# Low parts of all expert weights on VectorE, indirect transfers alone on GpSimd

## The chip, the cores and the metric

The kernel runs on one core of one Trainium2 chip. The metric is the device time of one execution in microseconds (us), the median of several runs.

## The reference

One decoder block over 2048 tokens of width 1024, in float32: RMSNorm, one input projection, dilated-window attention beside an mLSTM, an output projection, a cross-attention to 256 memory tokens, a mixture of experts, and a final norm. The change touches the mixture of experts. A router gives each token one of four groups and two of the four experts in it. Cut to what matters:

```
glog, elog -> g_idx, top_i, e_w                    # group, two experts, two weights
xb = h_pad[row_tok].reshape(nblk, 128, D)          # tokens sorted by expert
y  = (silu(xblk @ w1[e]) * (xblk @ w3[e])) @ w2[e] # w1, w3: 1024x512, w2: 512x1024
out = zeros.at[row_tok].add(y * row_w)
x  = rms_norm(x + out, g_final)
```

## The kernel before, in words

**Three products for one.** A float32 product is made from three matmuls on a shorter float type (fp32r). Each operand is split into a high part (a cast, on ScalarE) and a low part (operand minus high part, a subtraction of two SBUF tiles). `split` (lines 35 to 44) issues both: line 38 is the cast on ScalarE, line 39 the subtraction on the engine that the caller names. For token tiles that come out of PSUM with a gain, lines 41 and 42 do the same; line 42 reads one PSUM and one SBUF tile, always on VectorE. So in the profile every "L39" instruction is a low part: on weights (128x512 each), or on the gated activations (`actl`).

**An expert.** `experts` (from line 1532) treats 16 experts in order of their token counts, counted from 0 here; expert j has room for C tokens, CAPS = 256 eight times, then 272, 288, 288, 320, 320, 352, 352, 384. For each expert:
- `gather`: indirect transfers on GpSimd's queue fetch token rows to tiles X.
- `turn`: PE transposes X by 128x128 blocks (line 1576), and lines 41 and 42 split the result to xh and xl, eight tiles.
- `up(q)`, q = 0 and 1: for each of two blocks f of 128 features, 24 matmuls with w1 and 24 with w3 (lines 875 to 877) into PSUM tiles `pa`, of which there are four; then silu on ScalarE (line 1628), the product `s` on VectorE (line 1629, which frees the two PSUM tiles), and the split to acth and actl (line 1630). An `up(q)` has 2 x 2 x 24 = 96 matmuls.
- `down`: for each tile of up to 128 tokens, two halves c of 12 matmuls of 512 columns (lines 1640 to 1642), scaled to y on ScalarE (c = 0, line 1644) or VectorE (c = 1, line 1646), and added to the result in memory by an indirect transfer on GpSimd's queue (line 1654). The last two experts fetch, add, norm and store rows instead (`update`).

**The weights.** A unit is 128 partitions of 2048 elements: w1 or w3 for one q (tiles ww_0 and ww_1 in the profile, the number is q), or half of w2 (w_0, w_1). `unit` (line 1581) loads 1 MB over SyncE's queue into one of the `raw` buffers, and calls `split` four times, 512 columns each. Four high and four low unit tiles exist, so a unit's tile comes free as PE finishes the unit four before. In `w13` w1's low parts are on GpSimd and w3's on VectorE; in `w2` half 0 is on GpSimd and half 1 on VectorE. Each expert so has 12 weight low parts on either engine. The weights of the next expert are formed while PE works on this one.

**The first expert** is known early. Its w1 and w3 for q = 0 and its w1 for q = 1 are loaded into buffers of the router (`raws`, tile leadw in the profile). The `lead` branch (lines 1590 to 1596) forms both parts of w1, q = 0, on GpSimd.

**What sets the order.** Each engine runs its instructions in one order, fixed when the program is built by a planner that simulates a time line (line 1867) with its own costs, priority by place in the program. `issue_after` puts instructions behind a given one on its own engine: the next expert's weights for q stand behind the split of the last activation of `up(q)` on ScalarE and VectorE.

Of the kernel before, what the change touches and what calls it, by code (L numbers as in the profile page):

```python
# [16 lines left out]
D = 1024  # L17
# [1514 lines left out]
def experts(tc, I, Z, router, out):  # L1532
    nc = tc.nc
    SP_ = mybir.EngineType.SP
    it = router.finish()
    with ExitStack() as ctx:
# [12 lines left out]
        class Expert:  # L1549
# [51 lines left out]
            def w13(self, q, raws=(None, None)):  # L1601
                cs = slice(q * 256, q * 256 + 256)
                return [self.unit(f"w{m}{self.j}_{q}", I[m][bass.ds(self.e, 1), :, cs].rearrange("o (k p) f -> p (o k) f", p=P), [KT, 256], eng, raw, q == 0 and raw is not None)
                        for m, eng, raw in (("w1", nc.gpsimd, raws[0]), ("w3", nc.vector, raws[1]))]

            def w2(self, q):
                return self.unit(f"w2{self.j}_{q}", I["w2"][bass.ds(self.e, 1), q * 256:q * 256 + 256, :].rearrange("o (k p) d -> p (o k) d", p=P),
                                 [2, D], (nc.gpsimd, nc.vector)[q])

            def up(self, q, w13):  # L1610
                j, C = self.j, self.C
                if q == 0:
                    self.act = [sp.tile([P, 4, self.nt * P], F32R, name=f"act{m}{j}", tag="act" + m, bufs=1) for m in "hl"]
                    if C < self.nt * P:
                        for a in self.act:
                            nc.vector.memset(a[:, :, C:].bitcast(F32), 0.0)
                act = self.act
                for f in range(2):
                    fs = slice(f * P, f * P + P)
                    ps = []  # L1620
                    for m, (wh, wl) in enumerate(w13):
                        p = pa.tile([P, 384], F32, name=f"pa{j}_{q}{f}{m}", tag="a")
                        for k in range(KT):
                            xh, xl = self.xt[k]
                            mm3(nc, p[:, :C], wh[:, k, fs], wl[:, k, fs], xh[:, :C], xl[:, :C], k == 0, k == KT - 1)
                        ps.append(p)
                    s_ = sp.tile([P, 384], F32, name=f"s{j}_{q}{f}", tag="silu")
                    nc.scalar.activation(s_[:, :C], ps[0][:, :C], AF.Silu)
                    nc.vector.tensor_mul(s_[:, :C], s_[:, :C], ps[1][:, :C])  # L1629
                    self.last = split(nc, act[0][:, 2 * q + f, :C], act[1][:, 2 * q + f, :C], s_[:, :C], nc.vector)  # L1630

            def weighted(self, w2, n, r):
                y = sp.tile([P, D], F32, name=f"y{self.j}_{n}", tag="y", bufs=6)
                for c in range(2):
                    ps = py.tile([P, 512], F32, name=f"py{self.j}_{n}{c}", tag="y")
                    cs, ns = slice(c * 512, c * 512 + 512), slice(n * P, n * P + P)
                    for f in range(4):
                        wh, wl = (t[:, f % 2, cs] for t in w2[f // 2])
                        ah, al = (t[:, f, ns] for t in self.act)
                        nc.tensor.matmul(ps, ah, wh, start=(f == 0), stop=False)  # L1640
                        nc.tensor.matmul(ps, ah, wl, start=False, stop=False)
                        nc.tensor.matmul(ps, al, wh, start=False, stop=(f == 3))
                    if c == 0:
                        nc.scalar.activation(y[:r, cs], ps[:r], AF.Copy, scale=self.rt[:r, n, 1:2])
                    else:
                        nc.vector.tensor_scalar(y[:r, cs], ps[:r], self.rt[:r, n, 1:2], None, op0=OP.mult)
                return y

            def down(self, w2):

                added = []
                for n, r in enumerate(self.rows):
                    y = self.weighted(w2, n, r)
                    d = nc.gpsimd.indirect_dma_start(out=Z["acc"], out_offset=bass.IndirectOffsetOnAxis(ap=self.ix[:r, n:n + 1], axis=0),
                                                     in_=y[:r], in_offset=None, compute_op=OP.add)
                    apart(tc, d, added)
# [45 lines left out]
        raws = router.raws + [None]  # L1702
# [168 lines left out]
```

## Time and profile before

| | us |
|---|---|
| median of 3 runs | 2247.65 (2243.78 to 2251.59) |
| the profiled execution's own time | 2247.41 |
| its span, first to last instruction | 2245.2 |
| busy: PE / PEld | 2050.7 / 1884.5 |
| busy: DVE / ACT / POOL | 1389.0 / 1044.3 / 886.2 |

DVE is VectorE, ACT ScalarE, POOL GpSimd, PE the matmuls and PEld the weight loads of TensorE. Times in the rows count from the span's start. A row of a time line is: start, length, engine, line, operation, out<-in, shape, count, and in brackets the idle time before it with what ended it. A row of a table of windows is: stretch, length, then busy time (and instruction count) of PE, PEld, DVE, ACT and POOL, the granted TensorE clock (1.00 is 2.4 GHz, 0.50 is 1.2 GHz), the DMA share and GB/s. Names that end in l are low parts, in h high parts, in r raw weights.

### The profile page before, as it was taken

How to read it: one execution, taken by the hardware profiler on the slowest of the kernel's cores; microseconds unless marked ns; L12 is line 12 of the kernel's file. 1: busy time of each engine (PE TensorE's matmuls, PEld its weight loads, DVE VectorE, ACT ScalarE, POOL GpSimd, SP SyncE). 2: the span in 40 equal slices, each digit the busy share in tenths (PEclk: the TensorE clock that was granted, in tenths of full speed). 3: DMA queues.
4: the chain of work that ended last, by engine and by line, in shares of the span. 5: the costliest groups of instructions: out<-in, count | busy, mean ns of one | idle time of the engine just before them, and what ended most of it. 6: DMA issues, size and time to landing. Idle time of an engine off the chain costs nothing. (4 is left out here: it accounts for less than half of the span.)

```text
span 2245.2 us, 36132 instructions
## 1 busy us (share of the span) xinstructions
PE 2050.7 (91%) x13247; PEld 1884.5 (84%) x13247; DVE 1389.0 (62%) x3127; ACT 1044.3 (47%) x2216; POOL 886.2 (39%) x603
## 2 busy tenths in 40 slices
PE   8999999999789898889788999849998999999995
PEld 6898988988678788889788999749888988889985
DVE  8125641254388888846787888765566656545487
ACT  5213431233267676656535454425544544444453
POOL 3541244411354545542320021155554645455433
PEclk9999999999999999999789999969999999999997
DMA  6553644432897888775631222367667666666686
GB/s 213 165 161 132 225 146 136 132 123 94 213 240 197 242 233 238 194 208 179 227 125 56 95 104 80 114 195 223 209 194 210 199 214 205 169 185 160 175 293 264
DMA packets 276244, 402.45 MB, mean 179 GB/s; under 512 B 28176, under 2 KB 204624, under 8 KB 276016
## 3 DMA queue, kind: packets, MB, share of 16 engines
q1 hardware_dynamic: 262528, 355.11, 51.1%
q0 software_dynamic: 13536, 45.00, 8.1%
q8 instruction: 106, 1.74, 0.3%
q14 instruction: 74, 0.61, 0.1%
HBM read 286.33 MB, written 114.00 MB: 178 GB/s over the span
## 5 line engine op out<-in xcount | busy, mean ns | idle before, releaser
L39 POOL TENSOR_TENSOR wl<-wr,wh 128x1024 fp32r<-128x1024 f32 (+1 forms) x46 | 118.9, 2607 | 256.4 <-ACT wh L38 222.0
L875 PE MATMUL pa<-xh,ww_1h 128*128 128x256 f32 (+5 forms) x512 | 156.3, 305 | 17.1 <-DVE s L1629 17.1
L876 PE MATMUL pa<-xl,ww_0h 128*128 128x256 f32 (+5 forms) x512 | 154.5, 310 | 7.1 <-DVE xl L42 7.1
L876 PE MATMUL pa<-xl,ww_1h 128*128 128x256 f32 (+5 forms) x512 | 155.1, 303 | 0.0
L877 PE MATMUL pa<-xh,ww_1l 128*128 128x256 f32 (+5 forms) x512 | 155.1, 303 | 0.0
L877 PE MATMUL pa<-xh,ww_0l 128*128 128x256 f32 (+5 forms) x512 | 147.8, 302 | 0.0
L334 PE MATMUL pn<-wh,xh 128*128 128x256 f32 (+1 forms) x512 | 144.9, 283 | 0.0
L335 PE MATMUL pn<-wl,xh 128*128 128x256 f32 (+1 forms) x512 | 144.9, 283 | 0.0
L336 PE MATMUL pn<-wh,xl 128*128 128x256 f32 (+1 forms) x512 | 144.9, 283 | 0.0
L875 PE MATMUL pa<-xh,ww_0h 128*128 128x256 f32 (+5 forms) x512 | 133.9, 302 | 3.1 <-ACT xh L41 1.8
L42 DVE SCALAR_TENSOR_TENSOR xl<-pt,f_gf,xh 128x256 fp32r<-128x256 f32 (+5 forms) x128 | 63.9, 513 | 99.4 <-ACT xh L41 91.4
L39 POOL TENSOR_TENSOR ww_0l<-ww_0r,ww_0h 128x512 fp32r<-128x512 f32 x60 | 83.5, 1428 | 102.9 <-ACT ww_0h L38 102.9
L41 ACT ACTIVATE xh<-pt,f_gf 128x256 fp32r<-128x256 f32 (+5 forms) x128 | 62.1, 500 | 129.7 <-PE pt L1576 109.1
L875 PEld LDWEIGHTS pa<-xh,ww_1h 128*128 128x128 f32 x512 | 100.9, 197 | 18.1 <-DVE s L1629 18.0
L39 POOL TENSOR_TENSOR ww_1l<-ww_1r,ww_1h 128x512 fp32r<-128x512 f32 x60 | 85.9, 1452 | 65.0 <-ACT ww_1h L38 37.0
L38 ACT CAST wh<-wr 128x1024 fp32r<-128x1024 f32 (+3 forms) x49 | 48.4, 1030 | 130.6 <-PE pn L336 58.0
L876 PEld LDWEIGHTS pa<-xl,ww_0h 128*128 128x128 f32 x512 | 99.0, 194 | 9.4 <-DVE xl L42 7.3
L39 DVE TENSOR_TENSOR ww_1l<-ww_1r,ww_1h 128x512 fp32r<-128x512 f32 x64 | 102.3, 1654 | 2.4 <-ACT ww_1h L38 2.3
L876 PEld LDWEIGHTS pa<-xl,ww_1h 128*128 128x128 f32 x512 | 100.8, 197 | 0.0
L877 PEld LDWEIGHTS pa<-xh,ww_1l 128*128 128x128 f32 x512 | 100.6, 196 | 0.0
L877 PEld LDWEIGHTS pa<-xh,ww_0l 128*128 128x128 f32 x512 | 98.2, 194 | 1.0
L335 PEld LDWEIGHTS pn<-wl,xh 128*128 128x128 f32 x512 | 97.1, 190 | 0.9
(710 smaller groups left out, 7365.1 us busy)
## 6 DMA issues: line engine op xcount, KB each, us to landing
ww_1r<-w SPq DMA_DIRECT2D x31, 1024.0 KB
ww_0r<-w SPq DMA_DIRECT2D x30, 1024.0 KB
wr<-w_in SPq DMA_DIRECT2D x43, 512.0 KB
w_0r<-w SPq DMA_DIRECT2D x16, 1024.0 KB
w_1r<-w SPq DMA_DIRECT2D x16, 1024.0 KB
z_v<-v SPq DMA_DIRECT2D x32, 256.0 KB
z_mqk<-mq SPq DMA_DIRECT2D x16, 512.0 KB
kk<-z_qkh SPq DMA_DIRECT2D x32, 256.0 KB
```

The lines of the kernel that those rows point to most:

```text
L38: a = nc.scalar.copy(hi, src)
L39: b = eng.tensor_sub(lo, src, hi.bitcast(F32))
L41: a = nc.scalar.activation(hi, src, AF.Copy, scale=scale)
L42: b = eng.scalar_tensor_tensor(lo, src, scale, hi.bitcast(F32), op0=OP.mult, op1=OP.subtract)
L334: nc.tensor.matmul(ps[:, :n], xhw, wh[:, k, :], start=(k == 0), stop=False)
L335: nc.tensor.matmul(ps[:, :n], xhw, wl[:, k, :], start=False, stop=False)
L336: nc.tensor.matmul(ps[:, :n], xlw, wh[:, k, :], start=False, stop=(k == KT - 1))
L875: nc.tensor.matmul(out, wh, xh, start=first, stop=False, skip_group_check=True)
L876: nc.tensor.matmul(out, wh, xl, start=False, stop=False, skip_group_check=True)
L877: nc.tensor.matmul(out, wl, xh, start=False, stop=last, skip_group_check=True)
```

## The change

Every low part of expert weights outside the `lead` branch is issued on VectorE. GpSimd keeps w1, q = 0, of the first expert (the lead branch, high and low part) and the indirect transfers. ScalarE's casts, the loads, the buffers, PE's matmuls and the text order are untouched; the planner fixes the order of the instructions anew.

```diff
@@ -1601,11 +1601,11 @@
             def w13(self, q, raws=(None, None)):
                 cs = slice(q * 256, q * 256 + 256)
                 return [self.unit(f"w{m}{self.j}_{q}", I[m][bass.ds(self.e, 1), :, cs].rearrange("o (k p) f -> p (o k) f", p=P), [KT, 256], eng, raw, q == 0 and raw is not None)
-                        for m, eng, raw in (("w1", nc.gpsimd, raws[0]), ("w3", nc.vector, raws[1]))]
+                        for m, eng, raw in (("w1", nc.gpsimd if q == 0 and raws[0] is not None else nc.vector, raws[0]), ("w3", nc.vector, raws[1]))]
 
             def w2(self, q):
                 return self.unit(f"w2{self.j}_{q}", I["w2"][bass.ds(self.e, 1), q * 256:q * 256 + 256, :].rearrange("o (k p) d -> p (o k) d", p=P),
-                                 [2, D], (nc.gpsimd, nc.vector)[q])
+                                 [2, D], nc.vector)
 
             def up(self, q, w13):
                 j, C = self.j, self.C
```

## Rows read from the trace of the kernel before

**Rows 1.** Windows: the expert stretch, all engines.

```profile
1491.60:2224.00 732.40, 696.80 (x4352) 639.50 (x4352) 437.88 (x669) 355.43 (x714) 364.82 (x274) 0.97 0.69 209
```

**Rows 2.** Windows: experts 2 to 7, then 14 and 15, from up's end to up's end.

```profile
1568.20:1607.40 39.20, 36.78 (x261) 33.88 (x260) 22.69 (x30) 20.32 (x43) 21.67 (x16) 1.00 0.70 210
1607.40:1650.30 42.90, 37.33 (x255) 34.87 (x254) 27.30 (x30) 21.11 (x45) 21.61 (x17) 0.96 0.65 193
1650.30:1688.10 37.80, 36.95 (x262) 34.01 (x261) 21.57 (x30) 19.30 (x41) 20.58 (x16) 1.00 0.75 230
1688.10:1731.60 43.50, 38.17 (x254) 35.72 (x253) 27.24 (x30) 21.60 (x46) 22.31 (x18) 0.92 0.70 202
1731.60:1768.40 36.80, 36.44 (x262) 33.98 (x261) 22.27 (x30) 19.50 (x42) 20.85 (x16) 1.00 0.69 205
1768.40:1810.60 42.20, 37.79 (x255) 35.36 (x253) 27.36 (x30) 20.54 (x44) 21.45 (x17) 0.92 0.65 190
...
2092.70:2142.70 50.00, 50.00 (x290) 46.76 (x289) 28.51 (x46) 26.45 (x51) 19.32 (x14) 1.00 0.63 188
2142.70:2206.80 64.10, 57.61 (x290) 53.15 (x289) 56.84 (x119) 35.57 (x68) 21.55 (x16) 0.92 0.77 278
```

**Rows 3.** Waits of PE in that stretch: us in total, times, longest.

```profile
PE pa L875 <- DVE s L1629: 18.0, 5, 4.4
PE pa L876 <- DVE xl L42: 7.1, 1, 7.1
```

**Rows 4.** Time line of DVE in expert 5.

```profile
1707.36 12.59 DVE L39 TENSOR_TENSOR ww_1l<-ww_1r,ww_1h 128x512 fp32r<-128x512 f32 x4
1719.88 0.74 DVE L1629 TENSOR_TENSOR s<-s,pa 128x256 f32<-128x256 f32 x2
...
1725.73 2.50 DVE L39 TENSOR_TENSOR w_1l<-w_1r,w_1h 128x512 fp32r<-128x512 f32 x4 [4.21 <-ACT w_1h L38]
```

**Rows 5.** Time lines of ACT and of PE there.

```profile
1710.37 0.39 ACT L1628 ACTIVATE s<-pa 128x256 f32<-128x256 f32 x1 [1.48 <-PE pa L877]
...
1720.34 0.58 PE L875 MATMUL pa<-xh,ww_1h 128*128 128x256 f32 x1 [4.31 <-DVE s L1629]
```

**Rows 6.** Time line of POOL there.

```profile
1706.72 3.81 POOL L39 TENSOR_TENSOR ww_1l<-ww_1r,ww_1h 128x512 fp32r<-128x512 f32 x3
1710.70 1.87 POOL L1654 DMA_INDIRECT z_acc<-y,ix  x1 [0.17 <-issue]
...
1713.29 5.51 POOL L39 TENSOR_TENSOR w_0l<-w_0r,w_0h 128x512 fp32r<-128x512 f32 x4
```

**Rows 7.** Tile ww_1l on DVE: shortest, median and longest low part in ns.

```profile
L39 DVE TENSOR_TENSOR ww_1l<-ww_1r,ww_1h x64: 675/1082/7754, 1516.6 to 2190.4; 128x512 fp32r<-128x512 f32 x64
```

**Rows 8.** Groups of DVE: line 42, which reads PSUM and one SBUF tile.

```profile
L42 DVE SCALAR_TENSOR_TENSOR xl<-pt,f_gf,xh 128x256 fp32r<-128x256 f32 x64 | 29.3, 478 | 37.2 <-ACT xh L41 29.2 <-issue 7.9
```

**Rows 9.** Windows of line 39 alone: DVE busy (count), POOL busy (count).

```profile
1491.60:2224.00 732.40, 261.03 (x252) 260.46 (x188) 0.97 0.69 209
```

**Rows 10.** Windows: one up(1) at C = 256 twice, then C = 352 and 320.

```profile
1595.70:1607.40 11.70, 11.70 (x100) 11.70 (x98) 8.44 (x10) 5.86 (x14) 6.64 (x5) 1.00 1.02 313
...
1713.00:1731.60 18.60, 14.29 (x100) 14.09 (x99) 11.63 (x12) 5.86 (x13) 7.18 (x7) 0.82 0.78 221
...
2127.10:2142.70 15.60, 15.60 (x100) 15.58 (x99) 10.34 (x22) 12.31 (x25) 7.05 (x5) 1.00 1.02 371
...
1978.80:1993.00 14.20, 14.20 (x100) 14.19 (x98) 5.41 (x9) 8.60 (x19) 7.92 (x7) 1.00 0.89 291
```

**Rows 11.** Time lines of DVE and POOL in the first expert.

```profile
1511.03 4.57 DVE L1561 CAST ix<-rt 128x3 int32<-128x3 f32 x1 [1.56 <-DMA rt<-z_rt]
...
1510.65 4.92 POOL L39 TENSOR_TENSOR ww_1l<-leadw,ww_1h 128x512 fp32r<-128x512 f32 x4
```

**Rows 12.** Time line of DVE in the last expert.

```profile
2181.30 3.54 DVE L1684 SCALAR_TENSOR_TENSOR fx<-fx,fvf,gfin 128x1024 f32<-128x1024 f32 x2
2184.75 6.35 DVE L39 TENSOR_TENSOR ww_1l<-ww_1r,ww_1h 128x512 fp32r<-128x512 f32 x4
```

**Rows 13.** Waits of DVE, and of PE on ACT, in the expert stretch.

```profile
DVE w_1l L39 <- ACT w_1h L38: 21.7, 9, 4.2
...
PE pa L875 <- ACT xh L41: 1.8, 2, 1.1
```

## The prediction on record

> **What bounds the kernel now.** I read the table of windows first, stage by stage. In the expert stretch, 732.4 us long, PE is busy for 696.8 us [rows 1], and most experts run without a pause: an expert of 256 tokens at its best takes 36.8 us with PE busy for 36.4 of them at clock 1.00 [rows 2]. So the stretch is PE's, and what the change can give is what PE loses beside that. The list of PE's waits names it: 18.0 us in five waits on the product s (line 1629) and 7.1 us in one wait on xl [rows 3], both VectorE's. Neither is long work in itself; both stood late in VectorE's queue.
>
> The time line of one such place shows why. In expert 5 the four w3 low parts begin at 1707.36 and take 12.59 us together; s follows at 1719.88 [rows 4]. The silu that s needs had ended at 1710.37 + 0.39 = 1710.76, and PE stood still for 4.31 us until 1720.34, that is from 1716.03 on [rows 5]. The same four subtractions take 2.50 us at 1725.73 [rows 4], when GpSimd does no low parts. During the 12.59 us GpSimd ran its own: the rest of ww_1l, an indirect transfer, and four of w_0l, ending at 1713.29 + 5.51 = 1718.80 [rows 6]. VectorE's last one gets through only after that. A low part of ww_1l on VectorE takes between 675 and 7754 ns [rows 7]; 7.75 us is more than the whole run of four on GpSimd. Line 42, which reads PSUM and only one SBUF tile, shows no such spread: 478 ns in the mean over the first eight experts [rows 8]. So: a VectorE instruction with two SBUF operands (and in one place a small copy within SBUF, [rows 11]) stands still while GpSimd works through a run of subtractions.
>
> Here a page differs from the row. The Trainium skill (SBUF — State Buffer, "Who interferes with whom") says that a VectorE instruction with two SBUF inputs contends with a GpSimd instruction that reads SBUF, and that the one that starts first holds the pair of ports for its whole instruction. That names the right pair. But by it VectorE would get in after each GpSimd instruction, so a low part would wait for one of them, and four low parts would be done in about 4 x (5.51/4 + 2.50/4) = 8.0 us (an estimate, lengths from rows 4 and 6): s at 1715.4, before PE stops, and no wait to remove. The rows show 12.59 us, and the measurement decides; what the rule would make of the time is the second rival below.
>
> **The change, part by part.** *Removed:* GpSimd's 188 low parts in the stretch, 260.5 us of its time [rows 9]. *Added:* the same 188 on VectorE. There are 252 of line 39 on VectorE now (188 on weights, 64 on activations) for 261.0 us [rows 9]. At the undisturbed 2.50/4 = 0.625 us [rows 4] the 376 weight low parts cost 235 us, and the 64 on activations about 0.45 us each, 29 us (an estimate: below the 0.478 us of line 42 at 256 columns, a bit above for the wider ones). That is 264 us against 261: VectorE's busy time in the stretch stays at some 438 us of 700 [rows 1], although it does twice the low parts.
>
> *Moved, wait by wait.* (a) Experts 2 to 7. Against 36.8 us the six windows are 2.4, 6.1, 1.0, 6.7, 0.0 and 5.4 us longer [rows 2], 21.6 us in all. Three of them hold a wait of about 4.3 us each [rows 3, 5] and the clock that fell with it: in the stalled up(1) 18.6 us against 11.7 us, so 2.6 us beyond the wait, at granted clock 0.82 against 1.00 [rows 10]. After the change eight low parts (5.0 us) from 1707.36 end at 1712.4; even if the four of w_0l stand before s too it runs at 1714.9, before 1716.03. I take the whole 21.6. (b) Experts 8 to 14 show no loss (expert 14: 50.0 us, PE busy 50.0 [rows 2]): nothing to gain. (c) The first expert: a CAST of three columns takes 4.57 us beside GpSimd's w1 low parts of 4.92 us [rows 11], and xl behind it keeps PE for 7.1 us [rows 3]. These low parts now stand on VectorE behind the last xl, so the CAST is short again: 4.4 us back, and of the clock some 1 us, since a wait of 2.7 us (for the list transfers before the CAST) stays: 5.4. (d) The last expert: 64.1 us [rows 2]. Clean it would be the 50.0 of expert 14 and two ups that are 15.6 - 14.2 = 1.4 us longer each for 32 columns more [rows 10], 52.8; so 11.3 us are lost. VectorE is busy for 56.8 us there [rows 2], with the final norm in the same queue. Without GpSimd's low parts it gets back 6.35 - 2.50 = 3.9 us [rows 4, 12] and something on the norm, which two instructions pass in 3.54 us there [rows 12], and it takes 12 x 0.625 = 7.5 us more. VectorE is nearly full there, so I take half, 5.6; bounds 0 and 11.3.
>
> *New waits.* VectorE's queue is in order, so a low part that waits for its cast holds what stands behind it. The trace has that already: nine waits of w_1l, the longest 4.2 us [rows 13], and PE lost nothing by them in the windows without loss. ScalarE makes a cast about as fast as VectorE takes it away, so a unit's four low parts end about one step after its last cast, earlier than the 5.5 us that GpSimd took [rows 6], and raw buffers come free earlier. I charge 2.6 us for small waits of the kind that PE shows on ScalarE now (1.8 us, [rows 13]) and keep 0 and 20 (1.3 us an expert) as bounds. GpSimd's transfers only lose what stood before them.
>
> Sum: 21.6 + 5.4 + 5.6 - 2.6 = 30 us off the profiled execution's 2247.4 (span 2245.2; its time is 0.2 us from the median): **2217 us**.
>
> **Rivals.**
> 1. *VectorE's order becomes the bound (slower).* Place: s in each up(1), behind eight ww_1l (5.0 us) and a wait for w_1's cast as long as the longest, 4.2 us [rows 13]. Slack is 1716.03 - 1710.76 = 5.3 us, so PE stands 3.9 us, with the clock 2.6 more (as in (a)): 6.5 us an expert. It decides from six experts on (6 x 6.5 = 39 against the 32.6 won); with nine of 15 it gives 2247.4 - 32.6 + 58.5 = 2273, with all 15 2312. For it: the order comes from a planner whose costs the trace doesn't show, and 24 low parts an expert now share one queue with s and xl. Against: the best expert has VectorE busy for 22.3 us with 12 low parts [rows 2], and 12 more at 0.625 make 29.8 of 36.8.
> 2. *The two engines pass the ports after each instruction, and the stalls have another cause.* Then the three long waits and the last expert's stay and only the small losses go, 2.4 + 1.0 + 5.4 = 8.8: 2239. Against: 7754 ns [rows 7], and the short CAST that stood still just as long as GpSimd's run [rows 11].
> 3. *Everything comes back*, the last expert too and no new wait: 21.6 + 6.6 + 11.3 = 39.5: 2208, some us lower if the last rows' transfers, no longer behind low parts, start sooner.
> 4. *The loads become the limit.* Stalled experts move 193 GB/s, clean ones 205, and one reached 230 [rows 2]. 43.5 us at 202 are 8.8 MB; at 230 that takes 38.2 us, 1.4 over the best. Over seven experts 10 us come off the gain: 2227.
>
> **The numbers.** Forecast 0.62 (2209 to 2232, with rival 4 inside its upper part), rival 3 0.13, rival 2 and a mixture with small new waits 0.13 (2232 to 2250), rival 1 0.12. Within 0.3%, which is 6.7 us and about what a measurement can tell, lies 2241 to 2254. Rivals 2 and 1 share it: same 0.06; slower 0.10; faster 0.84. The range reaches from 2200 (rival 3 with an earlier end) to 2246, which leaves rival 1 and a part of rival 2 outside.
>
> **What would show it.** Right: weight low parts on VectorE at 0.62 to 0.69 us each with no long ones; line 39 on VectorE near 264 us; PE's wait on s from 18.0 to under 4 us; the windows of experts 3, 5 and 7 near 37 us at clock 1.00; the first expert's CAST at 0.2 us. Wrong: PE waits on s or xl of over 3 us at more than five places, with VectorE's queue held by a low part whose cast is late; or low parts still over 1 us, which would mean that the indirect transfers disturb them as well.

## The result and the profile after

The changed kernel takes **2211.68 us** (median of 4 runs, 2205.8 to 2215.31); the kernel before took 2247.52 (4 runs, 2243.78 to 2251.59). The ratio is **0.9834 [0.9815, 0.9853]**: 35.8 us less, where 2217 was forecast. The profiled execution is the slowest of the four (2215.31 us, span 2213.5; before 2247.4 and 2245.2), so the rows below account for a span difference of 31.7 us.

The windows of the expert stretch after, cut where before's were (up's end to up's end): expert 0, then 2 to 7, 14 and 15, and last the whole stretch with what lies around it. Columns: the window, its length, busy us of PE, PEld, DVE, ACT and POOL, granted clock, DMA share, GB/s.

```profile
1496.30:1532.10 35.80, 30.01 (x213) 28.73 (x214) 19.93 (x53) 18.14 (x38) 10.21 (x11) 0.85 0.78 248
...
1567.90:1603.10 35.20, 35.20 (x254) 33.13 (x253) 20.30 (x40) 17.83 (x38) 5.62 (x4) 1.00 0.74 212
1603.10:1640.00 36.90, 36.72 (x262) 34.11 (x261) 23.64 (x44) 21.10 (x45) 5.48 (x4) 1.00 0.81 236
1640.00:1675.30 35.30, 35.30 (x254) 33.22 (x254) 21.54 (x42) 19.00 (x41) 5.60 (x4) 1.00 0.81 233
1675.30:1711.50 36.20, 36.20 (x261) 34.09 (x260) 24.59 (x46) 22.15 (x48) 5.41 (x4) 1.00 0.81 242
1711.50:1746.70 35.20, 35.20 (x254) 33.14 (x253) 22.51 (x43) 19.55 (x42) 5.51 (x4) 1.00 0.78 226
1746.70:1783.60 36.90, 36.90 (x264) 34.41 (x263) 22.46 (x43) 20.31 (x44) 5.48 (x4) 1.00 0.77 223
2064.10:2114.20 50.10, 50.10 (x290) 46.86 (x289) 27.62 (x59) 25.63 (x49) 4.94 (x3) 1.00 0.65 186
2114.20:2171.20 57.00, 54.59 (x289) 50.54 (x288) 48.95 (x135) 36.45 (x70) 3.35 (x4) 0.97 0.82 305
...
1490.00:2240.00 750.00, 686.93 (x4352) 631.04 (x4352) 432.73 (x909) 356.62 (x717) 124.26 (x97) 0.97 0.70 211
```

Against [rows 2], the 42.9, 43.5 and 42.2 us of experts 3, 5 and 7 have become 36.9, 36.2 and 36.9, with PE busy for all but 0.2 us of any of them, at clock 1.00. Nor did an expert between them keep its 36.8 to 39.2: they take 35.2 or 35.3.

Line 39 alone from the start of the stretch on (VectorE, GpSimd), to be held against [rows 9], and the tile ww_1l, against [rows 7]:

```profile
1496.30:2240.00 743.70, 262.29 (x440) 0.00 (x0) 0.98 0.70 212
```

```profile
L39 DVE TENSOR_TENSOR ww_1l<-ww_1r,ww_1h x124: 616/682/721, 1520.3 to 2150.1; 128x512 fp32r<-128x512 f32 x124
```

Twice the low parts (376 of weights, not 188, beside the 64 of activations) cost VectorE about the same time, 262.29 us for 261.03, since the longest of ww_1l now takes 0.72 us and not 7.75. The time line of VectorE in expert 5, where [rows 4] showed 12.59 us, then in the first and the last expert ([rows 11, 12]):

```profile
1512.20 0.17 DVE L1561 CAST ix<-rt 128x3 int32<-128x3 f32 x1 [0.26 <-DMA rt<-z_rt]
...
1691.17 1.90 DVE L39 TENSOR_TENSOR ww_1l<-ww_1r,ww_1h 128x512 fp32r<-128x512 f32 x3 [3.76 <-ACT ww_1h L38]
...
1695.03 2.49 DVE L39 TENSOR_TENSOR ww_1l<-ww_1r,ww_1h 128x512 fp32r<-128x512 f32 x4
1698.69 0.42 DVE L1629 TENSOR_TENSOR s<-s,pa 128x256 f32<-128x256 f32 x1 [1.17 <-ACT s L1628]
...
2141.75 2.47 DVE L1684 SCALAR_TENSOR_TENSOR fx<-fx,fvf,gfin 128x1024 f32<-128x1024 f32 x2
```

Now s waits for its own silu (1.17 us, expert 5), not for a low part. PE's waits in the stretch, in total, times and longest, against [rows 3]:

```profile
PE pt L1576 <- DMA X<-z_h,ix: 9.9, 2, 8.2
PE pt L1576 <- DVE xl L42: 2.4, 1, 2.4
PE pa L876 <- DVE xl L42: 2.2, 1, 2.2
PE py L1640 <- DVE fv L1681: 2.2, 1, 2.2
...
PE py L1640 <- ACT acth L38: 1.4, 1, 1.4
```

The 18.0 us on s are gone and the 7.1 on xl are 2.2. The 9.9 us at the head is the first gather of X before the first expert; the kernel before has that wait too (8.4 us), and it doesn't explain where the stretch starts: the run that starts first of all (1481.2) has 10.0 us of it.

Where the span went, by stage (us; the start is PE's first transpose of the stage, an expert ends with the last matmul of its second up, the tail runs from the last up's end to the span's end). Most of the experiments discussed below stand in the same table, worked out in the same way from their traces:

```
                    start    e0    e1   e2-7  e8-14   e15   tail
before             1491.6  41.2  35.3  242.5  332.1  64.0   38.5
after              1496.3  35.8  35.8  215.7  330.6  57.0   42.3
control (= after)  1486.1  36.8  35.8  215.1  330.6  55.4   46.1
idle subs, w2      1488.9  42.5  35.8  215.5  330.6  57.8   46.4
memsets            1492.4  36.5  35.8  215.3  330.6  56.3   43.0
w1+w3 on VectorE   1481.2  41.5  35.8  215.1  330.6  56.8   47.3
w2 on VectorE      1487.7  40.9  35.3  226.3  333.8  59.1   44.7
idle subs, all     1490.3  40.3  35.8  232.5  339.1  59.4   50.6
before, own waits  1483.1  40.2  35.4  228.8  339.6  59.5   44.2
low parts twice    1483.0  35.5  38.8  225.4  333.0  58.5   48.9
```

From before to after: start -4.7, expert 0 +5.4, expert 1 -0.5, experts 2 to 7 +26.8, 8 to 14 +1.5, expert 15 +7.0, tail -3.8: 31.7, the span difference. The start scatters between 1481 and 1497 over all the profiles, at a stage that the change does not touch, so single spans are no measure of a few microseconds and the columns of the experts are. Two of the rows come from the fastest execution of their kernel: w1+w3 on VectorE (2210.04 us, median 2220.0) and low parts twice (2225.0, median 2233.85). They show 9 to 10 us less loss than the medians.

### The profile page after: what moved, and what is told of

Same layout as the page of the kernel before. It is cut to its first block, busy times and chain, and to the rows that moved or that the text cites. A ratio compares the mean times of both kernels' runs of the same rounds, so it can differ in the third digit from the quotient of the medians.

```text
span 2213.5 us, 36146 instructions
## 1 busy us (share of the span) xinstructions
PE 2041.5 (92%) x13247; PEld 1875.2 (85%) x13247; DVE 1373.3 (62%) x3315; ACT 1043.4 (47%) x2216; POOL 635.0 (29%) x415
## 5 line engine op out<-in xcount | busy, mean ns | idle before, releaser
L1654 POOL DMA_INDIRECT z_acc<-y,ix x34 | 55.9, 1645 | 407.2 <-DVE y L1646 175.5
L39 DVE TENSOR_TENSOR ww_1l<-ww_1r,ww_1h 128x512 fp32r<-128x512 f32 x124 | 77.6, 676 | 46.3 <-ACT ww_1h L38 46.2
L334 PEld LDWEIGHTS pn<-wh,xh 128*128 128x128 f32 x512 | 97.1, 190 | 0.9
L336 PEld LDWEIGHTS pn<-wh,xl 128*128 128x128 f32 x512 | 96.9, 189 | 0.5
```

What stands on the lines that cost most here:

```text
L39: b = eng.tensor_sub(lo, src, hi.bitcast(F32))
L334: nc.tensor.matmul(ps[:, :n], xhw, wh[:, k, :], start=(k == 0), stop=False)
L336: nc.tensor.matmul(ps[:, :n], xlw, wh[:, k, :], start=False, stop=(k == KT - 1))
```

## The experiments

Theory A: VectorE's two-input instructions are held while GpSimd subtracts; take GpSimd's subtractions away and the gain follows. Theory B: the gain comes from something else that the change moves (the planner's new order, low parts ready sooner, GpSimd's transfers no longer behind subtractions). Each experiment is the changed kernel with an edit, unless it says otherwise; its ratio is to the kernel before on the same chip.

**Control: the changed kernel itself.** No edit.

> The changed kernel once more, beside the next three on the same chip: ratio to the kernel before 0.983 to 0.986.

2209.45 us, 0.9856 [0.9819, 0.9892]. Line 39 takes

```profile
1490.00:2240.00 750.00, 262.24 (x440) 0.00 (x0) 0.98 0.69 209
```

**Idle subtractions on GpSimd.** After each low part of the unit, GpSimd subtracts the high part from itself into one scrap tile that nobody reads; VectorE's own work stays as it is.

```diff
+                        if name[:2] == "w1" or name[:2] == "w2" and name[-1] == "0":
+                            nc.gpsimd.tensor_sub(junk, f(h)[:, cs].bitcast(F32), f(h)[:, cs].bitcast(F32))
```

> The changed kernel, and beside it GpSimd subtracts each 512 columns of the high part of w1 and of the first half of w2 from themselves into a tile that nobody reads: as many subtractions of the same shape, at about the same places, as GpSimd had before the change. VectorE still forms every low part. Theory A (a VectorE instruction with two SBUF operands is held up while a run of GpSimd instructions reads SBUF): the weight low parts on VectorE go from 0.68 us to over 1 us in the mean with the longest over 4 us, PE waits on s and xl again, and the time goes back to 2240 us or above (up to 2275, since 24 low parts an expert are exposed in place of 12). Theory B (the gain came from the new order and from low parts being ready sooner than GpSimd made them): nothing waits for these subtractions, so the time stays at 2212 within 7.

A slip in the edit: w1's units are named "ww1...", so the first test never held, and the 64 subtractions ran for w2's first half only. 2213.66 us, 0.9872 [0.9842, 0.9901]. Line 39 on VectorE, then a place on both engines' time lines:

```profile
1490.00:2240.00 750.00, 301.92 (x440) 0.00 (x0) 0.97 0.69 209
```

```profile
1514.74 5.02 DVE L39 TENSOR_TENSOR ww_1l<-ww_1r,ww_1h 128x512 fp32r<-128x512 f32 x4
...
1513.09 5.51 POOL L1601 TENSOR_TENSOR junk<-w_0h 128x512 f32<-128x512 f32 x4 [5.80 <-ACT w_0h L38]
```

VectorE lost 40 us (301.92 against 262.24 in the control), but in even pieces: beside GpSimd's run three of the four low parts take about 1.52 us, starting and ending in turn with GpSimd's of 1.37 to 1.51, and none longer. That is handing over after each instruction, just what I had argued could not be. In experts 1 to 14 nothing is lost; expert 0 loses what the change had won there (42.5 us against 36.8), with PE waiting 4.4 us for s. So handing over is cheap where s has time to spare, and the long holds need something more. One thing differs from the kernel before besides the place: all these subtractions write one scrap tile, and each starts 0.08 us after the end of the one before, where GpSimd's low parts overlap.

**Writes alone.** The same places (and the same slip), two memsets of the raw tile, some 0.53 us each, in place of the subtraction.

```diff
+                            for _ in range(2):
+                                nc.gpsimd.memset(f(raw)[:, cs], 0.0)
```

> The changed kernel, and beside it GpSimd writes zeros twice over each 512 columns of the raw weights of the same units, after their low part is formed: GpSimd is busy in the same places, but reads nothing. Theory A in its narrow form (only reads of GpSimd hold VectorE up): low parts stay at 0.68 us and the time at 2212 within 7, at most some us more since a raw buffer comes free a little later. Theory A in its wide form (any run of GpSimd does): low parts over 1 us and 2240 or above, as with the subtractions. Theory B: 2212 to 2225, by the later buffers.

2207.87 us, 0.9839 [0.9805, 0.9872]; line 39 takes 262.42 us, and no ww_1l is over 0.715 us. 85 low parts ran beside a memset, the longest for 0.69 us. So at w2's places neither GpSimd's writing nor its being busy holds VectorE; what the subtraction adds is that it reads. Memsets right behind an indirect transfer, where the long holds turn out to stand, were not tried.

**One half of the change, and the other.** First only w1 moves and GpSimd keeps w2's first half (64 low parts); then only w2 moves and GpSimd keeps w1 (124).

```diff
-                                 [2, D], nc.vector)
+                                 [2, D], (nc.gpsimd, nc.vector)[q])
```

> Only w1's low parts are moved to VectorE; w2's first half stays on GpSimd (64 of the 188). Theory A: one run of four subtractions (5.5 us) an expert is left, beside ww_1l or w_1l; a low part can wait 5.5 us but not 7.7; most of the gain stays, 2215 to 2232, longest low part 4 to 6 us. Theory B: the part of the gain goes with the share of the moved low parts, 124 of 188: 2224.

```diff
-                        for m, eng, raw in (("w1", nc.gpsimd if q == 0 and raws[0] is not None else nc.vector, raws[0]), ("w3", nc.vector, raws[1]))]
+                        for m, eng, raw in (("w1", nc.gpsimd, raws[0]), ("w3", nc.vector, raws[1]))]
```

> Only w2's first half is moved to VectorE; w1 stays on GpSimd (124 of the 188). Theory A: the long wait in experts 3, 5 and 7 came from ww_1l and w_0l back to back; without w_0l VectorE's four ww_1l end about 5.5 us earlier, before PE stops, so these three waits go (18 us), the first expert's CAST and the last expert's wait stay: 2222 to 2236. Theory B: 64 of 188 of the gain, 12 us: 2235, with waits of PE spread over all experts.

With w1 moved: 2220.0 us, 0.9902 [0.987, 0.9934]; experts 2 to 7 take 215.1 us as in the control, although GpSimd still subtracts for 91.5 us. With w2 moved: 2229.73 us, 0.9943 [0.9918, 0.9967]; experts 2 to 7 take 226.3. Of the 27.4 us that they lose in the kernel before against the control, w2's low parts alone on GpSimd so cost nothing, w1's alone 11.2, and the rest comes only with both. A place in the second of these kernels, VectorE and GpSimd, and PE's waits in it:

```profile
1622.65 7.18 DVE L39 TENSOR_TENSOR ww_1l<-ww_1r,ww_1h 128x512 fp32r<-128x512 f32 x3
...
1621.08 0.96 POOL L1565 DMA_INDIRECT X<-z_h,ix  x1 [0.30 <-PE py L1642]
1622.06 3.84 POOL L39 TENSOR_TENSOR ww_1l<-ww_1r,ww_1h 128x512 fp32r<-128x512 f32 x3
1626.07 1.88 POOL L1654 DMA_INDIRECT z_acc<-y,ix  x1 [0.17 <-issue]
```

```profile
PE pa L876 <- DVE xl L42: 6.4, 1, 6.4
PE pt L1576 <- DVE xl L42: 5.7, 6, 1.2
PE pa L875 <- ACT xh L41: 4.7, 5, 1.4
```

The first of the three low parts begins at 1622.65 and ends at 1626.46, after GpSimd's whole run (to 1625.90): held through, not handed over. What stands before that run is an indirect transfer. I went through every trace with this in mind. For each run of GpSimd subtractions (under about 0.1 us between them) I asked whether it begins within 0.1 us of an indirect transfer, and by how much the VectorE instructions beside it exceeded their own undisturbed length (those over 0.15 us; count, longest and sum in us):

```
                   behind an indirect transfer     not behind one
before                20    7.08    74.9            61   1.17   55.2
idle subs, w2          -                            56   0.92   45.8
w1+w3 on VectorE       -                            40   1.18   34.3
w2 on VectorE         13    4.64    32.1            54   1.17   49.0
before, own waits     50    5.90    62.5            45   1.16   39.0
idle subs, all       169    5.27   108.5            94   0.54   42.1
control                -                             -
```

Away from indirect transfers no hold is longer than one GpSimd instruction (1.3 us, or some 0.58 where it is 256 wide). Only in a run that began right behind one is VectorE ever held through two or more; in the kernel before such a hold ends with the run, at most 0.56 us after it. With w2's low parts alone on GpSimd, or idle subtractions in their place, every run begins 1.3 us or more after the last transfer. In the kernel before w1's come first, and then w2's stand right behind a scatter too, in experts 2 to 10: nine runs, and in each of them one hold of 3.5 to 7.1 us. This is where both halves together cost more than each alone.

**Idle subtractions for w1 too.** The names put right, each subtraction cut in two of 256 columns with an output of its own, so that GpSimd's instructions need not wait for each other. All real low parts stay on VectorE.

```diff
+                        if name[:3] == "ww1" or name[:2] == "w2" and name[-1] == "0":
+                            for n2 in range(2):
+                                s2 = slice(i * 512 + n2 * 256, i * 512 + n2 * 256 + 256)
+                                nc.gpsimd.tensor_sub(junk[:, n2], f(h)[:, s2].bitcast(F32), f(h)[:, s2].bitcast(F32))
```

> The first experiment had its idle subtractions only beside the first half of w2 (64 of 128x512), so the ones beside w1 are missing there; here GpSimd subtracts beside w1 too, each 512 columns as two halves, into two halves of a tile that nobody reads. All real low parts stay on VectorE. The traces so far split by what GpSimd did just before a run of subtractions: behind an indirect transfer VectorE was held for up to 7.1 us beyond an instruction's own time (20 cases in the kernel before), otherwise for 1.2 us at most (61 cases there, 56 in the first experiment). Theory A2 (only runs right behind an indirect transfer hold VectorE for the whole run, and only these cost time): w1's idle subtractions stand behind indirect transfers again, so VectorE low parts of over 3 us come back, PE waits on s, and the time is 2230 to 2260. Theory A1 (ports pass after every instruction, long waits had another cause): no low part over 2 us, time 2212 to 2222. Theory B (order and earlier weights): 2212 within 7.

2249.93 us, 1.0036 [1.002, 1.0052]: **the whole gain is gone**, though every low part that is used is made where the change makes it. Line 39 on VectorE; one place on VectorE, GpSimd and PE; and PE's waits:

```profile
1490.00:2240.00 750.00, 388.05 (x440) 0.00 (x0) 0.97 0.69 209
```

```profile
1642.65 5.67 DVE L39 TENSOR_TENSOR actl<-s,acth 128x256 fp32r<-128x256 f32 x1 [0.47 <-ACT acth L38]
...
1643.43 4.61 POOL L1603 TENSOR_TENSOR junk<-ww_0h 128x256 f32<-128x256 f32 x8
...
1648.38 0.50 PE L1647 MATMUL py<-w_1h,actl 128*128 128x512 f32 x1 [2.25 <-DVE actl L39]
```

```profile
PE pt L1577 <- DVE xl L42: 12.7, 8, 2.1
PE py L1647 <- DVE actl L39: 6.8, 5, 2.2
PE pa L876 <- DVE xl L42: 6.8, 1, 6.8
```

One actl of 0.41 us takes 5.67: it sits there through GpSimd's eight subtractions and ends 0.28 us after them, and PE stops for 2.25 us. I had expected the weight low parts to be over 3 us again; they reach 2.04, and the long ones are five: four actl of 5.6 to 5.7 and a CAST of 3.70. The runs that hold the four actl began right behind a scatter, but 10 to 12 us earlier, and VectorE had taken its turns in them until then. And the largest of PE's waits, 12.7 us on xl, is not of the long kind. In expert 3 four low parts take their turns with GpSimd ahead of xl, for 3.83 us instead of 2.5, and PE waits:

```profile
1608.03 3.83 DVE L39 TENSOR_TENSOR ww_0l<-ww_0r,ww_0h 128x512 fp32r<-128x512 f32 x4
1611.78 0.86 DVE L42 SCALAR_TENSOR_TENSOR xl<-pt,f_gf,xh 128x256 fp32r<-128x256 f32 x2
...
1612.30 0.44 PE L1577 MATMUL pt<-ident,X 128*128 128x128 f32 x2 [1.87 <-DVE xl L42]
```

Theory A in its strong form (contention is enough) holds; where it would strike, and that only long holds cost time, was wrong.

**Before, with GpSimd made to pause.** The kernel before; each GpSimd low part but a unit's first also covers the last column of the one ahead of it, and so must wait for that write. No other work is changed.

```diff
+                    elif eng is nc.gpsimd and i:
+                        nc.scalar.copy(f(h)[:, cs], f(raw)[:, cs])
+                        lap = slice(i * 512 - 1, i * 512 + 512)
+                        eng.tensor_sub(f(l)[:, lap], f(raw)[:, lap], f(h)[:, lap].bitcast(F32))
```

> The kernel before, with GpSimd forming its 188 low parts as before, but each of a unit's second to fourth subtraction also recomputes the last column of the one before (513 columns), so that GpSimd has to wait for its own write before it starts the next: the runs are no longer back to back. Theory A2: VectorE gets in between, no low part of VectorE over about 3 us, PE's three long waits in experts 3, 5 and 7 go, and much of the gain comes without a move: 2215 to 2232. Theory B (GpSimd's low parts are late by themselves, or their place in the order costs): 2240 to 2255, since GpSimd's subtractions only get slower.

2233.67 us, 0.9952 [0.9936, 0.9968]. One row of the tile, PE's wait on s, VectorE's time line in expert 3, and the windows of experts 3, 5 and 7:

```profile
L39 DVE TENSOR_TENSOR ww_1l<-ww_1r,ww_1h x64: 676/1210/6574, 1508.1 to 2171.7; 128x512 fp32r<-128x512 f32 x64
```

```profile
PE pa L875 <- DVE s L1633: 2.5, 1, 2.5
```

```profile
1615.67 6.37 DVE L39 TENSOR_TENSOR ww_1l<-ww_1r,ww_1h 128x512 fp32r<-128x512 f32 x4
1621.97 0.74 DVE L1633 TENSOR_TENSOR s<-s,pa 128x256 f32<-128x256 f32 x2
```

```profile
1595.30:1633.00 37.70, 36.22 (x254) 33.52 (x253) 22.56 (x31) 21.16 (x46) 22.56 (x17) 1.00 0.78 225
...
1673.10:1711.60 38.50, 36.41 (x253) 33.11 (x253) 23.82 (x34) 21.25 (x45) 22.39 (x17) 1.00 0.71 208
...
1751.50:1787.40 35.90, 35.73 (x255) 33.42 (x254) 22.57 (x30) 19.44 (x42) 22.22 (x17) 1.00 0.78 227
```

The three long stalls of experts 3, 5 and 7, 13.1 of the 18.0 us on s, are gone; the 2.5 us left stand in the last expert. VectorE's order in expert 3 is that of [rows 4], four ww_1l and then s, but the four take 6.37 us. One long hold is left, 6.57 us, in a run in which the low parts of two units alternate, so that each has its write behind it and they overlap again. Experts 3, 5 and 7 got back 16.5 of the 18.6 us that the change gives them ([rows 2] and the windows after), with the low parts still on GpSimd. Experts 4 and 6 became slower, so that experts 2 to 7 as a whole got 13.7 of 26.8, and experts 8 to 14 lost 7.5 (339.6 for 332.1). So a pause between GpSimd's instructions lets VectorE in, and the long holds were nearly all of what the stalled experts lost; the held time as a whole fell only from 130 to 101 us.

**VectorE's own time.** In place of GpSimd's idle work VectorE makes the 188 low parts a second time, into a scrap tile.

```diff
+                        if name[:3] == "ww1" or name[:2] == "w2" and name[-1] == "0":
+                            nc.vector.tensor_sub(junk, f(raw)[:, cs], f(h)[:, cs].bitcast(F32))
```

> The changed kernel, and VectorE forms each of the 188 moved low parts a second time into a tile that nobody reads: 188 x 0.625 = 118 us more of VectorE's own time, as much as the 124 us by which GpSimd's idle subtractions of the fifth experiment lengthened line 39 on VectorE (388.1 against 264.3 us), but without GpSimd, and known to the planner. If VectorE's time as such is what costs, the time goes to about 2245 as there. If it is that single instructions in front of s and xl are held at moments that the planner did not plan for, VectorE's room (29.8 of 36.8 us in a short expert, so 7 us spare against 7.5 more) takes most of it: 2212 to 2230.

2233.85 us, 0.9968 [0.9955, 0.9982]. The stretch, and PE's waits in it:

```profile
1490.00:2240.00 750.00, 683.79 (x4327) 627.15 (x4325) 530.92 (x1073) 356.56 (x714) 121.02 (x90) 0.97 0.69 209
```

```profile
PE pa L876 <- DVE xl L42: 9.1, 5, 2.2
PE pa L875 <- ACT ww_0h L38: 3.0, 3, 1.5
```

Nothing is held (no ww_1l over 0.72 us), yet most of the gain is lost: VectorE's time is not free, as a pure theory of holds would have it. 104 us more of it (530.92 against the control's 426.81) cost about 24 us, 0.23 each; the idle subtractions added 136 us (562.57) and cost about 40, 0.30 each. But VectorE's sum doesn't rank the kernels by itself: before it is 447.89 at ratio 1, with the w2 idle subtractions 469.22 at 0.9872. There the extra time is spread in pieces under 1 us; in the kernel before three pieces of 7 us stood ahead of s.

**Four that looked for more.** w1's lead unit of the first expert on VectorE as well; the y of the last two experts all on ScalarE; and 4 or 8 of the final norm's 8 pairs of rows ahead of the last expert's last weight load, for 6 (the expectations say gather).

```diff
-                        for m, eng, raw in (("w1", nc.gpsimd if q == 0 and raws[0] is not None else nc.vector, raws[0]), ("w3", nc.vector, raws[1]))]
+                        for m, eng, raw in (("w1", nc.vector, raws[0]), ("w3", nc.vector, raws[1]))]
```

> The changed kernel with the last GpSimd subtractions moved too: w1, q = 0, of the first expert is split by ScalarE and VectorE behind the router's last step. VectorE does four low parts (2.5 us) more before the first matmuls, but these wait for the gathered rows about 8 us longer anyway: 2212 within 7 by every theory; a gain would show that GpSimd's lead work had held the router's small VectorE steps up.

```diff
-                    if c == 0:
+                    if c == 0 or self.j in (14, 15):
```

> The changed kernel with the second half of y of the last two experts scaled on ScalarE in place of VectorE (six instructions of 0.75 us). In the changed kernel PE's last waits (2.4, 1.4, 0.8, 2.2 us) stand in these two experts, where VectorE also forms the final norm. If VectorE's load there is what is left, 2 to 6 us come off: 2206 to 2210; if the order of its queue is, no change.

```diff
-FINAL = 6
+FINAL = 4
```

> The changed kernel with 4 instead of 6 of the 8 final row pairs ahead of the last expert's gather: VectorE's norm work in the last expert moves later. If the last waits of PE (2.4 us at its start, about 5 us in its down) come from norm work in front of them, 0 to 5 us come off or move to the tail: 2207 to 2218.

The same line with 8:

> The changed kernel with all 8 final row pairs ahead: VectorE is free of them before the last expert's down and the tail, but the first half of that expert is fuller: 2205 to 2216, below the control only if the waits in down (1.4, 0.8, 2.2 us) weigh more than the one at the start.

0.9868 [0.9841, 0.9896], 0.9843 [0.9818, 0.9869], 0.9867 [0.9838, 0.9896] and 0.986 [0.9826, 0.9893] against the control's 0.9856 [0.9819, 0.9892]: no difference in any. The tail stays 42.4 to 47.8 us long in all four, so what made it longer than before's 38.5 is located (four waits in the last expert's down, 4.8 us in the profile after; two of them on VectorE, for fv 2.18 and actl 0.76) but not mended, and no version beats the changed kernel.

## Why the prediction was right

**The cause** was right: GpSimd's subtractions hold VectorE's two-input instructions, and with them gone s is on time. Idle subtractions alone take the whole gain back. By itself that would not tell holds from VectorE's time, since 104 us more of its own work cost 24 us; the pauses do, which cut the stalls of experts 3, 5 and 7 with the low parts left where they were. What I had concluded about the manner was half right. I read from [rows 4 to 7] that VectorE stands still through a whole run of subtractions. That happens only in runs that begin behind an indirect transfer, and not to every instruction beside those; elsewhere GpSimd hands over after each instruction. In expert 5 the z_acc scatter of [rows 6] stood right there, and I named it only in passing.

So the Trainium skill's rule (SBUF — State Buffer, "SBUF: two separate sides"), that the first to start holds the shared pair for its whole instruction, describes 61 of the 81 holds in the kernel before (the longest 1.17 us); the other 20, up to 7.08 us, go past it, and they hold more than half of the 130 us. The Trainium skill's statement (SBUF — State Buffer, "Who interferes with whom") that a GpSimd instruction which only writes doesn't contend with one of VectorE's with two SBUF inputs agrees with the memsets (262.42 us against 262.24).

**Line 39 on VectorE**: 264 forecast, 262.29 measured; GpSimd's share was free indeed.

**(a) Experts 2 to 7**: 21.6 forecast, 26.8 measured. The mis-sized term is the baseline. I took 36.8 us for an expert without a loss; that one had GpSimd's low parts too. The six take 35.95 in the mean (215.7 / 6), and 6 x 0.85 = 5.1 accounts for the 5.2 more. A best case seen under the load to be removed is not the floor without it.

**(b) Experts 8 to 14**: 0 forecast, 1.5 measured. Expert 14, from which I judged the seven, was clean; expert 8 was not (41.2 to 38.4 us), and expert 9 lost 1.3.

**(c) The first expert**: 5.4 forecast, 5.4 measured (41.2 to 35.8; the control's takes 36.8), and by the step named: the CAST takes 0.17 us, not 4.57, and the wait on xl fell by 4.9 us. The five kernels with GpSimd subtractions beside it take 40.2 to 42.5, the one with memsets 36.5. (Rival 3 puts it at 6.6 us and doesn't say why.)

**(d) The last expert**: 5.6 forecast, half of what was lost; measured 7.0. The norm's two instructions fell from 3.54 to 2.47 us, the low parts from 1.6 to 0.68 each. But the tail behind it, for which the sum had no term, gave back 3.8, so the end as a whole brought 3.2 (1.0 in the control). That (d) came out near half is luck: half was a guess between 0 and 11.3.

**New waits**: 2.6 forecast for small ones on ScalarE, spread over the stretch; measured 0.5 in expert 1 and the tail's 3.8, which sits at the very end, where VectorE has the norm, the last actl and y at once.

The signed terms, 21.6 + 5.4 + 5.6 - 2.6 = 30, came out as 26.8 + 1.5 + 5.4 + 7.0 - 0.5 - 3.8 = 36.4; the late start of this one profile (-4.7), which is not the change's, makes it 31.7. The medians moved by 35.8.

**The rivals.** The first (VectorE's order as the bound) did not come: in expert 5 s waits for its silu, with 1.17 us to spare in VectorE's queue, and VectorE is busy for 20.3 to 24.6 us of experts 2 to 7, not the 29.8 that I allowed: the 12 low parts that it had already got shorter too. It was nearer than I gave it credit for: 104 us more on VectorE bring PE five waits on xl. The second is refuted as a whole, since the stalls of experts 3, 5 and 7 go with the long holds, though its picture of passing the ports in turn is true of most holds. The third (2208) lies inside the spread of the runs; its size was right, its reasons only in part (the last expert kept 7 of its 14 us over the 50.0 of expert 14). The fourth (loads as the limit) fell: experts 2 to 7 move 212 to 242 GB/s after, against 190 to 230 in [rows 2], with no PE wait on a weight.

**What stays open.** Why a run behind an indirect transfer isn't interrupted. Overlap of GpSimd's own instructions is not it alone: in the kernel before they start 0.03 to 0.05 us ahead of the last one's end behind a gather of X, with holds through three of them, and 0.03 to 0.08 us away from transfers, with none. Behind a scatter, in the nine runs of experts 2 to 10, they overlap by 0.46 to 0.64 us, and so they do around the one long hold that the pauses left; where a self-wait puts 0.08 us between them, holds fall to about one instruction. Nor is the transfer next to every long hold: the actl of 5.6 to 5.7 us stand 10 us behind one. And experts 2 to 7 regain only 13.7 of 26.8 us once the long holds are gone: how much of the rest is the short holds, how much low parts that VectorE makes sooner than GpSimd's 1.3 us each, and how much the pauses themselves, no run separates.

## What to carry to other kernels

Work on an idle engine is not free if it holds a resource that the busy path uses: look at the longest case of an instruction beside its median (7754 against 675 ns here), then at what the other engine did in exactly that stretch and right before it. The sum of contention says little by itself. 40 us of it in pieces of under 1 us cost nothing in experts 1 to 14, where there was time to spare, and 5.7 us in expert 0, where there was not; 126 us of it, most of it in pieces, took the whole gain. One long hold ahead of an instruction with 5 us of slack costs PE the stall, and the clock after it. And take the floor of a stage from a stretch without the load that is to go, or say that you can't.

## What the runs showed of the hardware

- A GpSimd subtraction (two 128x512 inputs, 1.3 us) beside a VectorE one (0.68 us): taking turns, they need 1.37 to 1.51 and 1.52 us. In a run that began right behind an indirect transfer VectorE may get nothing until GpSimd's run is over: 3.81 us for a low part beside three subtractions, 7.75 us at the worst, 5.67 us for an actl of 0.41 (there 10 us after the transfer).
- It isn't only the wide ones: CASTs of 3 columns within SBUF took 4.57 us (before) and 3.70 us (idle subtractions) for 0.17.
- GpSimd memsets and indirect transfers by themselves lengthen no VectorE low part (at most 0.72 us in the control, with 90 GpSimd instructions in the stretch; at most 0.69 us beside a memset).
- A GpSimd subtraction that must wait for the one before it starts 0.08 us after that one's end, and PE's wait on s falls from 18.0 to 2.5 us; without such a wait it starts 0.03 to 0.08 us before that end, or 0.46 to 0.64 us before it behind a scatter.
